# Attention of a 2-layer hybrid decoder step: a hand-written round of tasks and a planner that puts tasks out by predecessors, buffers and engine times

## The chip, the core and the metric

The kernel runs on one core of a Trainium2 chip. The metric is device time in microseconds (us), from the first to the last instruction plus what lies around it; the time of a kernel is the median of its runs. The engines are TensorE (PE in the profile; PEld is its weight load), VectorE (DVE), ScalarE (ACT), GpSimd (POOL) and SyncE (SP), which issues nearly all DMAs. Each engine takes its instructions in the order in which the program put them out, and waits on semaphores for the others.

## The reference, cut to what matters

One inference step for 256 new prompt tokens and 8 sequences of 4 sample tokens with 2,048 tokens of paged cache: two layers, each between two half-step SwiGLU FFNs. Layer 0 mixes by a short convolution, layer 1 by native sparse attention, whose three branches are a softmax over compressed blocks, one over the selected blocks and one over a window:

```python
def nsa_attend(q, t_pos, gates, k_cmp, v_cmp, gather_sel, kv_win, s_win):
    ...
    p_c = jax.nn.softmax(jnp.where(m_c, s_c, NEG), axis=-1) * m_c
    o_c = jnp.einsum('bqkgn,bnkd->bqkgd', p_c.astype(q.dtype), v_cmp)
    ...
    score = jnp.where(forced, FORCE_BONUS, jnp.where(valid, imp, -FORCE_BONUS))
    _, idx = lax.top_k(score, min(TOP_N, nb_s))
    k_sel, v_sel = gather_sel(idx)
    ...
    p_s = jax.nn.softmax(s_s.reshape(B, Tq, N_KV_HEADS, GROUP, n_sel * L_SEL), axis=-1)
    ...
    p_w = jax.nn.softmax(jnp.where(m_w, s_w, NEG), axis=-1)
    o_w = jnp.einsum('bqkgs,bskd->bqkgd', p_w.astype(q.dtype), kv_win[:, :, 1])
    o = gates[:, :, 0, ..., None] * o_c + gates[:, :, 1, ..., None] * o_s + gates[:, :, 2, ..., None] * o_w
```

All values are float32. The kernel computes the large products as three products of a high and a low part (`whi`, `wlo` of the weights, `xh`, `xl` of the activations).

## The kernel before

Prompt and sample tokens lie side by side (288 columns) in all projections and FFNs. The only stage that the change touches is the attention, between the last projection (queries) and `attention_out`; ahead of it and behind it the kernel is the same.

The attention has two kinds of work. The **sample** part goes over 20 chunks: for each of 4 pairs of sequences the window (`"w"`) and 4 chunks of the paged cache (0 to 3), each chunk 2 loads of 1 MB, one for each sequence of the pair. A chunk takes scores on PE (`s_scores`, `mm<-early,Qbd` and the like), mask and maximum on DVE (L1234), the exponential on ACT (L1235), four transposes on PE (`s_turn_p`, `tr<-ident,S`), a copy out of PSUM on ACT (L1248) and the values on PE (`s_values`, `acc<-early,PTs`). Chunks 0 to 3 need a mask `mk`, which a rank on PE (`s_rank`, `tr<-pcs,G`) and a chain of small DVE instructions make for each pair; at a pair's end stand small steps that weigh and add the parts (`s_weights` to `s_out`). The **prompt** part goes over 8 units of two heads: scores in two halves (`prompt_scores`, `mm<-kT,qT`), 8 exponentials on ACT, a scaling on POOL, 12 transposes, three copies, and values (`prompt_values`, `acc<-PcT,VcBig` and `acc<-PA,V`, `acc<-PB,V`).

PSUM has 8 banks: 4 `mm`, 2 `tr`, 2 `acc`. Before the attention the PSUM pool is closed and opened again with the same counts.

The pages' loads go into 12 buffers: 4 of the ring `raw` (which holds weights elsewhere), 4 `early`, and 4 pairs `whi`/`wlo` of the ring of converted weights, these until load 30 of 40. A load is issued on SP when the values of the chunk that had its buffer are put out; behind the last page the weights of `attention_out` are loaded into `raw`.

The order is written out by hand: a start (`START`) and then for every chunk the same round (`ROUND`), in which `i` takes prompt steps from a list at a pace of 0.8, `p` and `v` are turn and values of this chunk, `s` the scores of the next, and 0, 1, 2 places for the small steps (`HOOKS`). Steps on ACT and DVE that follow a PE step are put out after a guessed time (`soon`, `spend`). Near the end of the prompt list two weights of `attention_out` are converted, high part on ACT (L158), low part on POOL instead of DVE (L159). In the last prompt unit the scaling is shared by POOL and DVE.

Of the kernel before, what the change touches and what calls it, by code (L numbers as in the profile page):

```python
# [53 lines left out]

START = 'sSiiRC'
ROUND = 'i0p1si2v'
PACE = 0.8
KEEP = (7, 4, 2)
HOOKS = ((-5, 1), (-3, 1), (3, 2), (4, 2), (5, 0), (5, 2))
PT_ACT = 1  # L60
EARLY = (2, 1)
# [4 lines left out]
def weight_chunks():  # L66
# [35 lines left out]
    yield from ffn("ffb", 1)  # L102

# [83 lines left out]
def tile_step(ctx, tc, x_turned, vectors, state_turned, cmp_pages, sel_pages, cache_win, win_pages, page_table,  # L187
# [540 lines left out]
    def nsa(at):  # L728
# [10 lines left out]
        enter.enter_context(psum_banks(mm=4, tr=2, acc=2))  # L739
# [260 lines left out]


        clock, due, ties = [0.0], [], count()

        def soon(t, f, key):
            heappush(due, (clock[0] + t, next(ties), f, key))

        def run():
            t, _, f, _ = heappop(due)
            now, clock[0] = clock[0], t
            f()  # L1010
            clock[0] = max(now, t)

        def spend(t):
            end = clock[0] + t
            while due and due[0][0] <= end:
                run()
            clock[0] = end

        def need(key):
            while any(w[3] == key for w in due):  # L1020
                run()

        units = {}

        def prompt_cmp(u):
            if not u:
                units["cs"] = accb()
            pv = units["cs"][:, :256].rearrange("p (a u x) -> p a u x", a=2, u=KD)
            for a in range(2):
                mm(pv[:, a, u], qT[:, u, a * P:(a + 1) * P], KcBD[:, u // 4], True, True)  # L1030
            if u < KD - 1:
                return
            s = A("pc", [P, 2, 16, 8])
            sv = units.pop("cs")[:, :256].rearrange("p (a h n) -> p a h n", a=2, n=8)
            nc.vector.tensor_tensor(s, sv, cmN[:, :, None, :].to_broadcast([P, 2, 16, 8]), op=OP.add)
            m = A("pcm", [P, 2, 16])
            nc.vector.tensor_reduce(m, s, AX.X, OP.max)
            nc.vector.tensor_tensor(s, s, m[:, :, :, None].to_broadcast([P, 2, 16, 8]), op=OP.subtract)
            soon(1.6, lambda: nc.scalar.activation(s, s, AF.Exp, scale=SCALE), "cmp")
            soon(2.2, lambda: prompt_cmp1(s, m), "cmp")  # L1040
            units["cmp"] = s

        def prompt_cmp1(s, m):
            nc.vector.tensor_reduce(m, s, AX.X, OP.add)
            nc.vector.reciprocal(m, m)

            gv = gN[:, :, 0:16].rearrange("p a (pr kp g) -> p a pr g kp", pr=2, kp=2)
            for pr in range(2):
                mv = m[:, :, pr * 8:(pr + 1) * 8].rearrange("p a (g kp) -> p a g kp", kp=2)
                nc.vector.tensor_tensor(mv, mv, gv[:, :, pr], op=OP.mult)  # L1050
            nc.vector.tensor_tensor(s, s, m[:, :, :, None].to_broadcast([P, 2, 16, 8]), op=OP.mult)
            nc.vector.tensor_tensor(s, s, cm01[:, :, None, :].to_broadcast([P, 2, 16, 8]), op=OP.mult)
# [19 lines left out]

        enter.close()
        enter.enter_context(psum_banks(**ATT))
# [4 lines left out]
        K = {1: kT[2], 2: kT[4]}  # L1079
        PcT = T("PcT", [P, NP])  # L1080

        def prompt_cmp2():
            need("cmp")
            s = units.pop("cmp")
            ps = trb()
            for a in range(2):
                tr(ps[:, a * P:(a + 1) * P], s[:, a].rearrange("p h n -> p (h n)"))
            spend(0.2)
            nc.vector.tensor_copy(PcT, ps[:, :NP])

        def prompt_scores(u, half):

            pr, g = divmod(u, 4)
            if half == 0:
# [397 lines left out]
```

## Time and profile before

| | us |
|---|---|
| median of 3 runs | 1292.18 (1290.5 to 1292.75) |
| the profiled execution | 1289.71 |
| its span | 1288.0 |
| PE busy | 1249.7 (97%) |
| DVE, ACT, POOL busy | 724.8 (56%), 583.6 (45%), 251.1 (19%) |
| attention, from its first own matmul to the first of `attention_out` | 906.48 to 1037.44 |
| PE busy in 906.4 to 1037.4 | 108.32 of 131.00 |

The busy time is the union of an engine's instructions. Matmuls overlap each other (the next one starts before the end of the one ahead), so a piece of PE work costs the distance from its start to the start of the next piece, which is a little less than the busy time printed beside it. "PEclk" is the granted TensorE clock, 1.00 for the higher of its two levels (2.4 GHz) and 0.50 for the lower (1.2 GHz); values between are a mean over the stretch.

### The profile page before, as it was taken

What the parts mean: (1) busy time and instruction counts of PE and PEld (TensorE: products, weight loads), DVE (VectorE), ACT (ScalarE), POOL (GpSimd) and SP (SyncE); (2) the same over time, 40 slices, a digit from 0 to 9 for tenths busy, and PEclk for the clock granted to TensorE, in tenths of its full rate; (3) what the DMA queues carried; (4) which work ended last, traced back from release to release, by engine and by line L of the source; (5) the groups of instructions that cost most, each with busy time, mean ns of one, the idle gap of its engine ahead of it and who ended that gap; (6) DMA issues with size and microseconds to landing.
All of it is one profiled execution on the core that took longest, in us unless ns stands there. A gap on an engine that the chain in (4) does not pass through costs nothing.

```text
span 1288.0 us, 26738 instructions
## 1 busy us (share of the span) xinstructions
PE 1249.7 (97%) x10679; PEld 1193.7 (93%) x10679; DVE 724.8 (56%) x1394; ACT 583.6 (45%) x1050; POOL 251.1 (19%) x264
## 2 busy tenths in 40 slices
PE   9999999999999999999999999999888799999997
PEld 9999999999999999999999999999555489999997
DVE  6654455665664544656554555665667556645553
ACT  6433335543553433445443444542566445433444
POOL 0250122222212101212211021310112032210211
PEclk9999999999999999999999999999899999999999
DMA  7755555655555456456544543775697836665432
GB/s 269 274 202 183 195 192 178 241 204 184 194 201 183 169 201 250 156 189 230 196 167 145 197 152 107 282 267 181 212 369 260 320 135 227 253 245 196 152 104 77
DMA packets 71598, 262.07 MB, mean 203 GB/s; under 512 B 7985, under 2 KB 9906, under 8 KB 56242
## 3 DMA queue, kind: packets, MB, share of 16 engines
q1 hardware_dynamic: 70450, 249.66, 54.6%
q0 software_dynamic: 256, 8.32, 1.7%
q10 hardware_dynamic: 768, 2.38, 0.5%
q8 instruction: 84, 1.38, 0.4%
q14 instruction: 40, 0.33, 0.1%
HBM read 257.31 MB, written 11.35 MB: 209 GB/s over the span
## 4 chain that ended last, share of the span: by engine, by line
PE 85%; DVE 5%; ACT 4%; issue 2%; POOL 1%; SPq 1%; DMA 1%; ACTq 0%; DVEq 0%; POOLq 0%
PE mm L218 75%; PE acc L218 9%; PE tr L249 2%; DVE wlo L159 2%; ACT whi L158 1%; SPq L922 1%; DVE S L1108 1%; ACT sq L311 1%; ACT L449 0%; POOL t L683 0%; POOL a L464 0%; DMA raw<-in_sel_pages_dram 0%; ACT S L1109 0%; DMA wlo<-in_sel_pages_dram 0%; DVE PA L1141 0%
## 5 line engine op out<-in xcount | busy, mean ns | idle before, releaser
L218 PE MATMUL mm<-xh,whi 128*128 128x288 f32 x1832 | 546.4, 298 | 2.1 <-DVE xl L1158 0.9
L218 PE MATMUL mm<-xh,wlo 128*128 128x288 f32 x1832 | 543.0, 297 | 1.0 <-DVE wlo L159 1.0
L218 PE MATMUL mm<-xl,whi 128*128 128x288 f32 x1832 | 536.0, 293 | 0.0
L159 DVE TENSOR_TENSOR wlo<-raw,whi 128x1024 fp32r<-128x1024 f32 (+2 forms) x360 | 405.0, 1138 | 120.1 <-ACT whi L158 118.8
L158 ACT ACTIVATE whi<-raw 128x1024 fp32r<-128x1024 f32 (+2 forms) x365 | 343.1, 953 | 87.2 <-PE mm L218 81.2
L218 PEld LDWEIGHTS mm<-xh,whi 128*128 128x128 f32 x1832 | 343.9, 188 | 5.5 <-issue 1.8
L218 PEld LDWEIGHTS mm<-xl,whi 128*128 128x128 f32 x1832 | 347.9, 190 | 0.5 <-DVE xl L305 0.2
L218 PEld LDWEIGHTS mm<-xh,wlo 128*128 128x128 f32 x1832 | 342.9, 187 | 2.1 <-DVE wlo L159 1.9
L218 PE MATMUL mm<-Ah,wlo 128*128 128x288 f32 x768 | 228.7, 298 | 1.7 <-DVE wlo L159 1.7
L218 PE MATMUL mm<-Ah,whi 128*128 128x288 f32 x768 | 228.2, 297 | 1.5 <-ACT Ah L467 1.0
L218 PE MATMUL mm<-Al,whi 128*128 128x288 f32 x768 | 227.4, 296 | 0.4 <-DVE Al L468 0.4
L464 POOL TENSOR_TENSOR a<-s,t 128x288 f32<-128x288 f32 x88 | 114.9, 1305 | 492.9 <-DVE t L462 318.4
L218 PEld LDWEIGHTS mm<-Ah,whi 128*128 128x128 f32 x768 | 145.2, 189 | 2.4 <-ACT Ah L467 1.2
L218 PEld LDWEIGHTS mm<-Ah,wlo 128*128 128x128 f32 x768 | 144.3, 188 | 3.1 <-DVE wlo L159 3.1
L218 PEld LDWEIGHTS mm<-Al,whi 128*128 128x128 f32 x768 | 144.6, 188 | 0.6 <-DVE Al L468 0.6
L467 ACT ACTIVATE Ah<-a 128x288 fp32r<-128x288 f32 x88 | 39.2, 445 | 143.9 <-POOL a L464 143.7
L460 ACT ACTIVATE s<-t 128x288 f32<-128x288 f32 x88 | 39.1, 445 | 141.8 <-DVE t L458 141.6
L462 DVE TENSOR_TENSOR t<-mm,rB 128x288 f32<-128x288 f32 x88 | 40.1, 456 | 90.8 <-PE mm L218 90.7
L468 DVE TENSOR_TENSOR Al<-a,Ah 128x288 fp32r<-128x288 f32 x88 | 40.7, 462 | 68.5 <-ACT Ah L467 68.5
L498 DVE SCALAR_TENSOR_TENSOR xT<-mm,xT 128x288 f32<-128x288 f32 x64 | 29.2, 456 | 83.1 <-PE mm L218 83.1
L218 PE MATMUL acc<-cp,W 128*64 128x128 f32 x1024 | 59.4, 274 | 0.0
L218 PEld LDWEIGHTS acc<-cp,W 128*64 128x64 f32 x1024 | 55.6, 137 | 2.8 <-issue 2.8
(287 smaller groups left out, 885.6 us busy)
## 6 DMA issues: line engine op xcount, KB each, us to landing
raw<-in_w_ffb_gu_dram SPq DMA_DIRECT2D x44, 1024.0 KB
raw<-in_w_ffa_gu_dram SPq DMA_DIRECT2D x42, 1024.0 KB
cp<-in_cmp_pages_dram SPq DMA_DIRECT2D x128, 256.0 KB
early<-in_sel_pages_dram SPq DMA_DIRECT2D x56, 256.0 KB
raw<-in_sel_pages_dram SPq DMA_DIRECT2D x56, 256.0 KB
raw<-in_w_ffa_down_dram SPq DMA_DIRECT2D x16, 768.0 KB
raw<-in_w_conv_in_dram SPq DMA_DIRECT2D x12, 1024.0 KB
raw<-in_w_ffb_down_dram SPq DMA_DIRECT2D x16, 768.0 KB
```

The costliest lines, as they stand in the source:

```text
L158: self.nc.scalar.activation(parts[0], v, AF.Copy)
L159: (lower or self.nc.vector).tensor_sub(parts[1], v, parts[0])
L218: nc.tensor.matmul(out, lhsT, rhs, start=start, stop=stop, skip_group_check=True)
L249: nc.tensor.transpose(out, in_, ident[:k, :k])
L311: nc.scalar.activation(sq, xT[:, d], AF.Square)
L460: nc.scalar.activation(s1, t1, AF.Silu)
L462: nc.vector.tensor_mul(t2, pu[:, :N], rB)
L464: nc.gpsimd.tensor_mul(a, s1, t2)
L467: nc.scalar.activation(Ah[:, f], a, AF.Copy)
L468: nc.vector.tensor_sub(Al[:, f], a, Ah[:, f])
L498: nc.vector.scalar_tensor_tensor(xT[:, d], py[:, :N], 0.5, xT[:, d], op0=OP.mult, op1=OP.add)
L922: nc.sync.dma_start(v[:, s:s + 1], sel_pages[bass.ds(at_[s0 + s], 1)].rearrange("s p c -> p s c"))
```

## The change

The hand-written order goes: `START`, `ROUND`, `PACE`, `KEEP`, `HOOKS`, the heap of guessed times. Each step of the attention becomes a `Task` with an engine, a time from a table (`TAKES`), predecessors, slots of buffer rings that it takes or uses, and a rank. `Plan.run` keeps a clock for each engine, finds the task that can begin first, among the tasks of its engine that can begin within 0.1 us of it takes the one of the lowest rank, and puts it out. Loads are tasks on a queue of their own, 3.0 us each. Sample chunk `c` has the rank `c`, prompt unit `u` 3 + 2.2 `u`. The PSUM pool stays open from the projections on. `S`, which holds a chunk's probabilities, gets 3 buffers instead of 2.

Four steps are computed another way: the weights of a pair (`weights`) are exponentials with a bias, two on ACT, without the two subtractions on DVE (L1280) and without the memset; the mask `okp` is multiplied in once at the end; POOL scales the smaller part of a prompt unit first, and does all of it in the last unit too; three weights of `attention_out` are converted ahead instead of two, all with POOL for the low part.

```diff
-START = 'sSiiRC'
-ROUND = 'i0p1si2v'
-PACE = 0.8
-HOOKS = ((-5, 1), (-3, 1), (3, 2), (4, 2), (5, 0), (5, 2))
-EARLY = (2, 1)
+RINGS = dict(mm=4, tr=2, acc=2, U=2, PA=1, PB=1, S=3, PTs=2, small=2, pc=1, score=1, mk=2, sum=2, PTm=2)
+TAKES = dict(
+    small=0.5, max=0.75, parts=0.95, share=0.35, rank=0.25, best=1.25, S=1.0, top=0.65, top_w=0.75, exp=0.75, turn=0.5, copy=0.5,
...
+LOAD, LAND, HOP, FIRST_PAGES = 3.0, 1.5, 0.12, 7
+SAMPLE, PROMPT, PROMPT0, NEAR = 1.0, 2.2, 3.0, 0.1
+EARLY = 3
...
+    def start(self, t):
+
+        at = self.free.get(t.engine, 0.0)
+        for x in t.after:
+            if x.end is None:
+                return None
+            at = max(at, x.end + (0.0 if x.engine == t.engine else HOP))
+        taken = {}
+        for s in t.slots:
+            n = taken[s.ring] = taken.get(s.ring, -1) + 1
+            last = self.rings[s.ring][n]
+            for x in last.users if last else ():
+                if x.end is None:
+                    return None
+                at = max(at, x.end + HOP)
+        return at
+
+    def run(self):
+        left = list(self.tasks)
+        while left:
+            able = [(self.start(t), t) for t in left]
+            able = [(at, t) for at, t in able if at is not None]
+            first, t0 = min(able, key=lambda x: x[0])
+            at, t = min((x for x in able if x[1].engine == t0.engine and x[0] <= first + NEAR), key=lambda x: x[1].rank)
+            left.remove(t)
+            for s in t.slots:
+                self.rings[s.ring] = self.rings[s.ring][1:] + [s]
+            t.end = self.free[t.engine] = at + t.takes
+            t.put()
...
-        enter.enter_context(psum_banks(mm=4, tr=2, acc=2))
+        psum = at_pages.enter_context(ExitStack())
+        psum.enter_context(psum_banks(mm=4, tr=2, acc=2))
...
         enter.close()
-        enter.enter_context(psum_banks(**ATT))
...
-            late = u == KD - 1
-            n = 2 if late else 4
-            nc.gpsimd.tensor_tensor(S1[:, :n], S1[:, :n], sm[:, 0:n, None].to_broadcast([P, n, NP]), op=OP.mult)
-            (nc.vector if late else nc.gpsimd).tensor_tensor(S0, S0, sm[:, 4:8, None].to_broadcast([P, 4, P]), op=OP.mult)
...
+            f0 = step("POOL", "f1", lambda: scale(1), [f], uses=[sl["U"]], rank=r)
+            f1 = step("POOL", "f0", lambda: scale(0), [f0], uses=[sl["U"]], rank=r)
...
-            nc.vector.memset(w[:, 0:1], 0.0)
-            for k, sl in ((1, slice(1, 3)), (2, slice(3, 8))):
-                nc.vector.tensor_reduce(m2[:, k:k + 1], nb[:, sl], AX.X, OP.min)
-                ts(w[:, sl], nb[:, sl], m2[:, k:k + 1], None, op0=OP.subtract)
-            soon(0.6, lambda: nc.scalar.activation(w, w, AF.Exp, scale=-1.0), ("w", i))
...
+            def weights():
+                for k, at_ in ((1, slice(1, 3)), (2, slice(3, 8))):
+                    nc.scalar.activation(t["w"][:, at_], t["nb"][:, at_], AF.Exp, scale=-1.0, bias=t["m2"][:, k:k + 1])
...
+        before = values_of[:PAGES["until"] // 2]
+        for n in range(EARLY):
+            def convert():
+                W.convert(nc.gpsimd)
+                plan.free["POOL"] = max(plan.free.get("POOL", 0.0), plan.free["ACT"]) + 2.4
+            before = [step("ACT", "whi", convert, [*before, loads[len(order) + n // 2]], rank=100.0)]
```

What the change moves is shown at three places. The first is PE at the attention's start, from the first pair's compressed scores (`KcT`) on; `pcs` is what the rank reads, `pc` the prompt's compressed probabilities. Before:

```order
L218 MATMUL acc<-KcT,Qbd 32x64 x4
L218 MATMUL acc<-kT_9640,Qbd 32x32 x4
L218 MATMUL acc<-kT_9639,Qbd 32x32 x4
L218 MATMUL mm<-early,Qbd 32x512 x4
L218 MATMUL mm<-kT_9639,qT 128x256 x2
L218 MATMUL mm<-kT_9640,qT 128x256 x2
L218 MATMUL mm<-kT_9639,qT 128x128 x2
L218 MATMUL mm<-kT_9640,qT 128x128 x2
L218 MATMUL tr<-pcs,G 128x64
L249 MATMUL tr<-ident,pc 128x128 x2
```

Now, on the same engine and from the same place:

```order
L278 MATMUL acc<-KcT,Qbd 32x64 x4
L278 MATMUL acc<-kT_9640,Qbd 32x32 x4
L278 MATMUL acc<-kT_9639,Qbd 32x32 x4
L278 MATMUL mm<-early,Qbd 32x512 x8
L278 MATMUL mm<-raw,Qbd 32x512 x8
L278 MATMUL tr<-pcs,G 128x64
L309 MATMUL tr<-ident,pc 128x128 x2
```

Ahead of the rank there are now the scores of four chunks instead of those of one chunk and of the first prompt unit.

The second place is PE in the middle, around the second pair's rank. Before, from the prompt scores ahead of it to the transposes of the chunk that needs its mask (the second `tr<-ident,S`):

```order
L218 MATMUL mm<-kT_9640,qT 128x256 x2
L249 MATMUL tr<-ident,S 128x128 x4
L218 MATMUL tr<-pcs,G 128x64
L218 MATMUL mm<-raw,Qbd 32x512 x4
L218 MATMUL acc<-raw,PTs 32x128 x16
L218 MATMUL mm<-kT_9639,qT 128x128 x2
L218 MATMUL mm<-kT_9640,qT 128x128 x2
L249 MATMUL tr<-ident,S 128x128 x4
L218 MATMUL mm<-whi,Qbd 32x256 x4
```

Now, from the same rank on (`S_10906` and `S_10905` are the two halves of a prompt unit, `Vc` and `Sel` small steps of the first pair):

```order
L278 MATMUL tr<-pcs,G 128x64
L278 MATMUL mm<-early,Qbd 32x512 x4
L278 MATMUL acc<-Vc,sq 32x128 x4
L309 MATMUL tr<-ident,S 128x128 x4
L309 MATMUL tr<-ident,S_10906 128x128 x4
L278 MATMUL acc<-Sel,rB 128x64
L278 MATMUL acc<-whi,PTs 32x128 x8
L278 MATMUL acc<-wlo,PTs 32x128 x8
L309 MATMUL tr<-ident,S_10905 128x128 x8
L278 MATMUL mm<-early,Qbd 32x512 x4
L278 MATMUL acc<-PcT,VcBig 128x256
L278 MATMUL acc<-PA,V_10091 64x256 x2
```

The transposes of the chunk with the new mask moved behind all of these and the rest of that unit's values; the `tr<-ident,S` seen here belongs to the window chunk, which needs no mask.

The third place is the end. On PE the last rows before `attention_out` (`mm<-xh,whi`) were those of the last prompt unit:

```order
L218 MATMUL acc<-Sel,rms 128x64
L249 MATMUL tr<-ident,S_11983 128x128 x4
L249 MATMUL tr<-ident,S_11982 128x128 x8
L218 MATMUL acc<-PcT,VcBig 128x256
L218 MATMUL acc<-PA,V_10091 64x256 x2
```

Now they are those of the last two chunks and of the last pair's small steps:

```order
L278 MATMUL acc<-early,PTs 32x128 x16
L278 MATMUL mm<-raw,Qbd 32x512 x4
L309 MATMUL tr<-ident,S 128x128 x4
L278 MATMUL mm<-raw,Qbd 32x512 x4
L278 MATMUL acc<-raw,PTs 32x128 x16
L309 MATMUL tr<-ident,S 128x128 x4
L278 MATMUL acc<-raw,PTs 32x128 x16
L309 MATMUL tr<-ident,ssm 128x128
L278 MATMUL acc<-Vc,sq 32x128 x4
L278 MATMUL acc<-Sel,rms 128x64
L278 MATMUL mm<-xh,whi 128x288
```

The prompt's pieces that stood between the sample's last steps moved ahead of the last two chunks. On ACT at the same place (`S,L` are chunk exponentials, `PTs` and `sq` copies, `wg` the pair's weights, `xh` the output's high part, `whi` weights of `attention_out`) there stands now:

```order
L1340 ACTIVATE S,L<-S,nb 128x512
L1365 ACTIVATE Og<-acc 128x128
L1393 ACTIVATE wg<-nb,m_12539 128x2
L1393 ACTIVATE wg<-nb,m_12539 128x5
L1349 ACTIVATE PTs<-tr 128x512
L1414 ACTIVATE sq<-tr 128x128
L218 ACTIVATE whi<-raw 128x1024
L1447 ACTIVATE xh<-acc 128x8x8
L218 ACTIVATE whi<-raw 128x1024 x3
```

The first conversion, which came between prompt copies before, moved to the place just ahead of the output's last high part, and three more stand behind it.

## Rows read from the trace of the kernel before

**Rows 1.** Stretches: length, busy PE, PEld, DVE, ACT, POOL, PEclk, DMA share, GB/s.

```profile
906.40:1037.40 131.00, 108.32 (x1430) 68.25 (x1430) 81.64 (x388) 80.19 (x269) 25.23 (x20) 0.96 0.77 276
932.60:1001.00 68.40, 57.30 (x818) 36.80 (x810) 46.95 (x226) 44.47 (x155) 14.59 (x12) 1.00 0.88 311
1001.00:1037.40 36.40, 29.32 (x360) 17.90 (x360) 17.95 (x70) 18.05 (x50) 4.80 (x3) 0.95 0.72 271
916.00:920.00 4.00, 4.00 (x40) 1.40 (x38) 3.25 (x23) 4.00 (x18) 0.97 (x1) 0.50 0.00 0
956.00:960.00 4.00, 4.00 (x62) 2.98 (x58) 0.96 (x4) 1.48 (x4) 0.53 (x2) 1.00 1.05 385
```

**Rows 2.** Waits of PE, 905 to 1038: us in total, times, longest.

```profile
PE tr L249 <- ACT S L1235: 5.6, 5, 1.3
PE tr L218 <- DVE pcs L1193: 3.6, 1, 3.6
...
PE tr L249 <- DVE mm L1228: 2.1, 1, 2.1
...
PE acc L218 <- DVE pc L1035: 0.5, 1, 0.5
```

**Rows 3.** PE in order of time, 925 to 937: start, busy, what [idle before].

```profile
925.07 1.07 PE L218 MATMUL mm<-raw,Qbd 128*32 128x512 f32 x8
926.06 0.70 PE L218 MATMUL acc<-PcT,VcBig 128*128 128x256 f32 x2
...
928.14 1.08 PE L218 MATMUL acc<-early,PTs 128*32 128x128 f32 x32
929.15 1.14 PE L218 MATMUL mm<-kT,qT 64*128 64x256 f32 x8
...
932.84 0.72 PE L218 MATMUL mm<-kT,qT 64*128 64x128 f32 x8
934.85 0.66 PE L249 MATMUL tr<-ident,S 128*128 128x128 f32 x4 [1.29 <-ACT S L1235]
...
936.44 1.09 PE L249 MATMUL tr<-ident,S 128*128 128x128 f32 x8
```

**Rows 4.** PE in order of time at the attention's start.

```profile
913.28 0.41 PE L218 MATMUL tr<-pcs,G 128*128 128x64 f32 x2 [3.63 <-DVE pcs L1193]
...
913.92 2.76 PE L218 MATMUL mm<-kT,qT 64*128 64x256 f32 x8
```

**Rows 5.** ACT in order of time at the attention's start.

```profile
908.15 1.28 ACT L1183 ACT_TABLE_LOAD   x1 [18.05 <-DVE mm L1228]
...
910.36 0.40 ACT L1039 ACTIVATE pc<-pc 128x256 f32<-128x256 f32 x1
910.67 0.71 ACT L1235 ACTIVATE S<-S,nb 128x512 f32<-128x512 f32 x1
```

**Rows 6.** ACT by line, 906.4 to 1037.4: busy us, mean ns, idle before.

```profile
L1109 ACT ACTIVATE S<-S,mx 128x256 f32<-128x256 f32 (+1 forms) x64 | 28.2, 443 | 2.9 <-DVE mx L1108 2.9
L1248 ACT ACTIVATE PTs<-tr 128x512 f32<-128x512 f32 x20 | 11.9, 593 | 8.8 <-PE tr L249 8.8
```

**Rows 7.** DVE in order of time beside POOL, third pair's weights.

```profile
996.43 1.38 DVE L1280 TENSOR_SCALAR wg<-nb,m 128x2 f32<-128x2 f32 x1
```

**Rows 8.** POOL in order of time, the same stretch.

```profile
995.89 1.89 POOL L1124 TENSOR_TENSOR S<-S,sm 128x1024 f32<-128x1024 f32 x1 [10.53 <-DVE sm L1121]
```

**Rows 9.** PE at the end: values of the last chunk but one, `attention_out` begins.

```profile
1018.41 1.07 PE L218 MATMUL acc<-raw,PTs 128*32 128x128 f32 x24
...
1037.44 0.40 PE L218 MATMUL mm<-xh,whi 128*128 128x288 f32 x1 [0.94 <-DVE xl L1158]
```

**Rows 10.** SP in order of time at the end: weights of `attention_out`.

```profile
1019.33 6.03 SPq L138 DMA_DIRECT2D raw<-in_w_nsa_out_dram  x4
```

**Rows 11.** ACT in order of time at the end: first conversion.

```profile
1032.02 1.05 ACT L158 ACTIVATE whi<-raw 128x1024 fp32r<-128x1024 f32 x1
```

**Rows 12.** POOL in order of time at the end: its low part.

```profile
1033.15 2.35 POOL L159 TENSOR_TENSOR wlo<-raw,whi 128x1024 fp32r<-128x1024 f32 x1 [1.01 <-ACT whi L158]
```

More of the change, by code (lines that the diff above doesn't have):

```diff
@@ L102, in weight_chunks, with __init__, add @@
     yield from ffn("ffb", 1)
+class Task:
+    def __init__(self, engine, takes, put, after=(), slots=(), uses=(), rank=0.0):
+        self.engine, self.takes, self.put, self.after, self.slots, self.rank = engine, takes, put, after, slots, rank
+        self.end = None
+        for x in (*slots, *uses):
+            x.users.append(self)
+class Slot:
+    def __init__(self, ring):
+        self.ring, self.users = ring, []
+class Plan:
+    def __init__(self, rings):
+        self.rings = {n: [None] * k for n, k in rings.items()}
+        self.free, self.tasks = {}, []
+    def add(self, *a, **k):
+        t = Task(*a, **k)
+        self.tasks.append(t)
+        return t
+    def start(self, t):
[25 more added lines that the diff above has]
+            t.put()
 class Weights:
@@ new lines, in nsa, with nothing, step, load_more @@
+        landed = {}
+        U = [(u, *divmod(u, 4)) for u in range(KD)]
+        groups = [(b2 * 2 + pr, b2, pr) for b2 in range(2) for pr in range(2)]
+        def nothing():
+            pass
+        def step(engine, name, put, after=(), slots=(), uses=(), rank=0.0):
+            return plan.add(engine, TAKES[name], put, after, slots, uses, rank)
+        loads = [Task("DMA", 0, nothing) for _ in range(len(order) + 2)]
+        queue = [0.0]
+        def load_more(at):
+            n = len(pages) + len(done) + W.loaded - W.attention
+            load_pages()
+            for k in range(n, min(len(pages) + len(done) + W.loaded - W.attention, len(loads))):
+                queue[0] = max(queue[0], at) + LOAD
+                loads[k].end = queue[0] + LAND
@@ L1389, in nsa @@
-        while prompt:
-            item()
-        while due:
-            run()
+            puts = []
+            for n in range(3):
+                x = Slot("tr")
+                p = step("PE", "pturn", lambda n=n: turn(n), [(f0, f1, f1)[n]], [x], [sl["U"]], r - 0.2)
+                puts.append(step("DVE" if n == 1 else "ACT", "copy_v" if n == 1 else "copy", lambda n=n: put(n), [p] + puts[:1],
+                                 {0: [sl["PA"]], 2: [sl["PB"]]}.get(n, []), [x] + [sl["PA"]] * (n == 1), r - 0.2))
@@ L1393, in nsa @@
+        for n, x in enumerate(loads[:len(pages)]):
+            x.end = queue[0] = max(0.0, LOAD * (n + 1 - FIRST_PAGES))
+        plan.run()
         W.bufs = RAW
```

575 lines of the change are left out of this document (278 added, 297 removed).

## The prediction

> **What bounds the kernel now.** I read the busy times first, then the stretches of the attention, then who PE waits for. PE is busy for 1249.7 of 1288.0 us (the table of the profile), so outside the attention nothing can be won by another order. In the attention it is busy for 108.32 of 131.00 us, DVE for 81.64, ACT for 80.19 and the DMA queues for 0.77 of the time [rows 1]: no engine is full, PE is the nearest to it, and 22.7 us of its time are idle. The idle time is many short waits: 5.6 us for a chunk's exponential, 3.6 us for the first rank, 2.1 us ahead of a pair's turn [rows 2].
>
> I need the work that PE must do. A piece costs the distance to the next start [rows 3]: a chunk's scores 926.06 - 925.07 = 0.99, its values 1.01, its four transposes 0.66 less the overlap of 0.07 = 0.59; a prompt unit's scores 1.07 and 0.72 - 0.07 = 0.65, its 12 transposes 1.5 x 1.09 = 1.6, its values 928.14 - 926.06 = 2.08. 20 chunks x 2.59 = 51.8, 8 units x 5.40 = 43.2, and I estimate the small steps of four pairs and the first turn at 6.5 together: 101.5 us. So 131 - 101.5 = 29.5 us are lost, in idle time and at the lower clock.
>
> By stretch, counting the pieces in PE's order against the same prices: up to 932.6, 26.2 us hold 18.8 of work (7.4 lost); from there to 1001, 68.4 us [rows 1] hold 56.8 (11.6 lost); to 1037.4, 36.4 us hold 25.9 (10.5 lost). The first contains the one long wait, 3.63 us up to 913.28, and behind it the same eight score matmuls take 2.76 us that take 1.14 later [rows 3, 4]: the granted clock is 0.50 from 916 to 920 [rows 1], its lower level. PE had been idle just before.
>
> **The start: about 4 us won.** PE now has the scores of four chunks (4 x 0.99) ahead of the rank. On ACT the first exponential comes now before the parts of the first pair; the table load of 1.28 us then begins after DVE's third instruction on `pc`, some 0.8 us before the 908.15 of now [rows 5], and the rank can begin at about 911.7 instead of 913.28. PE's own work lasts until about 910.8, so the 3.63 us shrink to about 1, and I expect no fall of the clock there. Then ACT sets the pace. Up to the copy that the fourth chunk's values need it must do table load, three parts, five chunk exponentials (0.71 [rows 5] plus the read of the sum, 0.82 each as an estimate), four copies of 0.59 [rows 6], eleven prompt exponentials of some 0.44 [rows 6] and small steps, 15.7 us in all; with 3 us of waits for DVE it gets there at about 926. Followed piece by piece, PE has put out 22.6 us of work by 932.6, six chunks and two prompt units of scores, against 18.8 before: 3.8 us won. The end on the low side is 1.6 (the earlier rank alone), on the high side 6 (the lead that the same walk shows at 921, if ACT does not eat a part of it).
>
> The open PSUM scope is worth at most the 0.5 us for which the first score matmul waited on DVE's read of the old bank [rows 2]; it is inside the start.
>
> **The middle: 6 us won of 11.6.** The waits for the exponential of 1.29 us each have one pattern: rank, one chunk's scores, values, half a unit, then transposes that need the rank's mask [rows 3], as the second place shown ahead has it. That is 1.0 + 1.0 + 0.65 us of PE work over a chain of rank, DVE mask, maximum and exponential that takes some 4 us. In the new order over 8 us of other pieces stand in between, and the copies have a whole piece beside them. The two subtractions on DVE go too; at the third pair the first of them took 1.38 us [rows 7], under a POOL scaling of 1.89 us [rows 8]. The Trainium skill (SBUF — State Buffer, Who interferes with whom) says that DVE and GpSimd share a port pair that is locked for a whole instruction; the two rows fit it. By that rule the five `tensor_scalar`s that stay in the pair's weights could each still be held up under a scaling, up to 1.9 us for three pairs, which the sum leaves out, since those weights are not wanted at once.
>
> What stays is not zero. The table's costs are mostly within 0.1 us of the rows (scores 1.0 for 0.99, values 1.0 for 1.01, prompt values 2.05 for 2.08), but transposes stand at 0.5 for 0.59 and copies at 0.5 for 0.59, and the engines can't leave the order. A chunk's chain is so 0.2 us longer than planned, and PE has only two `tr` and two `acc` banks to run ahead in. Bounds for what is still lost in the middle: 2 us (only the table's errors show) and 11.6 us (as now). I take 5.5, 0.35 us a piece over some 16 chunk and unit pieces that are close to their copies, nearer to the lower end because the plan has the same rows' durations. Won: 6.1.
>
> **The end: nothing won.** All prompt work now stands ahead of the last two chunks. From the end of chunk 18's scores: its mask, maximum and exponential (0.78 + 0.87) with PE idle, transposes, scores of chunk 19, values, transposes of 19 (0.65 idle), its copy (0.7 idle), values, then weights (2.0 on DVE), a turn, a copy, small values, three small sums, the output and its two parts: 11.2 us, estimated with the same prices and 0.2 to 0.3 us for each small step, of which PE works 5.3. Before, 10.5 us were lost in the last stretch; now 5.9. Two things take this back. First, weights: their load is issued when chunk 18's values free `raw`, as now [rows 9, 10]: values from 1018.41, issue at 1019.33. Now only about 7 us follow, where 18 did. Two loads at the best rate of the trace, 385 GB/s [rows 1], need 2.7 us each, so with a second or two of issue and flight the first `whi` (1.05 us [rows 11]) begins about 4.5 us after the values, ACT holds it ahead of the last `xh`, and POOL's low part (2.35 us [rows 12]) ends some 12.4 us after the scores of chunk 18: PE stands for 1.3 us more. With POOL doing three low parts in a row, 7.1 us, PE's 2.4 us a piece follow them without a further stop. Second, PE works 5.3 us of 12.5, about as little as before 913, so I expect the lower clock at the start of `attention_out`, at the price of 913.28 to 920, some 3 us. The Trainium skill (TensorE: Matmul & The Clock Gate, What's actually happening) has the slow clock as the resting state that activity lifts; it speaks against a tail without prompt work. It can also stay high, as it does in the middle with its waits of 1.29 us. Lost at the end: 5.9 + 1.3 + 3 = 10.2, against 10.5. Bounds: 5.9 and 14 (a weight landing 4 us late).
>
> **Loads.** 28 of the 40 loads are issued inside the attention, 5.45 us a chunk at 385 GB/s. By the walk the first chunk's buffers come free at about 916, the fourth's at 928, and the last page then lands at about 1000, while PE needs it at about 1013. So the loads hold nothing up, with some 12 us to spare; at the 311 GB/s of the middle now [rows 1] it would be just in time.
>
> **The sum.** 3.8 + 6.1 + 0.3 = 10.2 us. Against the profiled execution (1289.71, of which 1288.0 are span): 1279.5. The median of the runs is 2.47 above it: 1282.
>
> **The rivals.**
> *ACT's fixed order takes the place of the waits (slower).* ACT now carries 64 prompt exponentials (28.2 us [rows 6]) between the chunks' exponentials and copies, in an order computed from costs that are too short. If a chunk's copy stands behind two to four prompt exponentials that wait themselves, PE stops with both `tr` banks full. It decides from 15.7 us lost in the middle on, 1.1 us for each of the 14 chunks; at the 1.29 us of now [rows 3] each, 18 us are lost and the kernel comes to 1294 to 1297. For it: at the start ACT really is the bound by my walk. Against it: ACT is busy for 44.47 of 68.40 us in the middle.
> *Loads bind.* If freed buffers come no faster than now, the last scores stand just ahead of 1018.41 again [rows 9], followed by the new tail: 4 us won at most, 1288.
> *The order does nothing on balance.* The waits go elsewhere, the same 29 us are lost, within 2 us of 1292. For it: the order before also keeps PE at 84% of the middle.
> *The plan holds well.* 2 us lost in the middle, no lower clock: 3.8 + 9.6 + 3.3 = 16.7, 1275.5; with the full lead at the start 1273.
>
> **How the numbers follow.** Forecast (1278 to 1287) 0.44; the plan holds well (under 1278) 0.20; loads bind or a small gain (to 1289.6) 0.11; nothing on balance 0.12; ACT (slower) 0.13. A measurement of this kernel can tell about 0.2%, 2.6 us, from no change. Faster 0.75, same 0.12, slower 0.13. Range 1273 to 1294, which leaves out about one in ten on either side.
>
> **What would show it.** Start: the wait ahead of the first `pcs` rank near 1 us, PEclk 1.00 in the stretch 906 to 926 after its start. Middle: waits of PE on the exponential under 2 us in total, PE busy near 92%. End: idle time between the last two chunks' scores and transposes, `whi` ahead of the last `xh` waiting for a DMA, PEclk under 1 at the start of `attention_out`. Wrong would be: PE waiting on ACT copies all through (ACT rival), or on DMA of pages, or `attention_out` beginning later than 1030.

## The result, and the profile after

| | before | after |
|---|---|---|
| median of 4 runs, us | 1292.07 (1290.5 to 1292.75) | 1277.15 (1275.35 to 1278.81) |
| the profiled execution | 1289.71 | 1278.04 |
| its span | 1288.0 | 1276.3 |
| attention, to the first matmul of `attention_out` | 130.94 | 113.75 |
| from there to the last of its sums of squares (`acc<-ss,ones`) | 32.66 | 36.85 |
| all that follows | 217.90 | 218.20 |

The ratio after to before is 0.9886, 95% interval 0.9868 to 0.9904: 14.9 us faster, where 10 were forecast. The attention became 17.2 us shorter, and `attention_out` gave 4.2 us back. The starts of these stretches are read to 0.1 us, so their lengths are good to about 0.05 us.

The first view is the stretches of the kernel after: time, then busy us and instructions of PE, PEld, DVE, ACT and POOL, then PEclk, the DMA share and GB/s. The attention is cut at the end of the first prompt unit's values (932.20) and of chunk 18's scores (1009.80); the last rows lie in `attention_out`.

```profile
907.50:932.20 24.70, 22.45 (x359) 14.63 (x358) 21.60 (x105) 18.72 (x70) 3.06 (x3) 1.00 0.78 270
932.20:1009.80 77.60, 72.29 (x983) 47.90 (x981) 47.93 (x240) 54.83 (x188) 20.26 (x17) 1.00 0.93 330
1009.80:1021.25 11.45, 5.41 (x95) 3.26 (x91) 5.57 (x25) 5.11 (x13) 0.34 (x1) 1.00 0.54 203
...
1020.00:1024.00 4.00, 1.33 (x7) 0.98 (x6) 0.22 (x1) 3.67 (x5) 3.09 (x2) 0.71 1.02 430
1024.00:1028.00 4.00, 4.00 (x18) 4.00 (x18) 2.43 (x1) 0.23 (x1) 4.00 (x2) 0.50 0.74 258
1028.00:1032.00 4.00, 4.00 (x31) 4.00 (x30) 0.46 (x1) 0.12 (x1) 0.92 (x1) 0.93 0.93 342
```

The idle time of PE is the difference of the first two numbers: 2.25 us in the start, 5.31 in the middle, 6.04 in the tail. In the middle PE is busy for 93% of the time, where the stretch before had 57.30 of 68.40 us, 84% [rows 1]. The clock is at its higher level all through the attention; before it fell behind the first rank [rows 1, 4] and once more in the last stretch (PEclk 0.95 from 1001.00 on [rows 1]). It falls now at the beginning of `attention_out`, down to 0.50 from 1024 to 1028.

The waits of PE from 905 to 1060 after (us in total, times, longest):

```profile
PE acc L278 <- DVE rms L1437: 3.0, 2, 1.6
PE tr L309 <- ACT S L1340: 2.5, 2, 1.7
PE mm L278 <- POOL wlo L219: 1.5, 1, 1.5
PE acc L278 <- DVE rB L1437: 1.3, 2, 0.7
```

Against [rows 2]: the five waits on a chunk's exponential (5.6 us) are down to two, both in the tail, and the 3.6 us for the first rank are gone from the top of the list. No PE wait on a page's load is among the waits. PE's own rows (start, busy, idle before and its releaser) show the first rank, then the tail and the beginning of `attention_out`:

```profile
912.09 0.41 PE L278 MATMUL tr<-pcs,G 128*128 128x64 f32 x2 [0.67 <-DVE mm L1330]
...
1011.53 0.65 PE L309 MATMUL tr<-ident,S 128*128 128x128 f32 x4 [1.67 <-ACT S L1340]
...
1019.72 0.41 PE L278 MATMUL acc<-Sel,rms 128*128 128x64 f32 x2 [1.33 <-DVE rms L1437]
...
1021.25 0.40 PE L278 MATMUL mm<-xh,whi 128*128 128x288 f32 x1 [1.13 <-DVE xl L1449]
...
1023.32 0.61 PE L278 MATMUL mm<-xh,wlo 128*128 128x288 f32 x1 [1.53 <-POOL wlo L219]
```

The weights of `attention_out` come late, as the rows of SP, ACT, POOL and DVE show:

```profile
1014.08 4.20 SPq L198 DMA_DIRECT2D raw<-in_w_nsa_out_dram  x4
...
1019.77 1.06 ACT L218 ACTIVATE whi<-raw 128x1024 fp32r<-128x1024 f32 x1 [1.87 <-DMA raw<-in_w_nsa_out_dram]
...
1020.91 8.01 POOL L219 TENSOR_TENSOR wlo<-raw,whi 128x1024 fp32r<-128x1024 f32 x3 [17.01 <-ACT whi L218]
...
1024.26 2.43 DVE L219 TENSOR_TENSOR wlo<-raw,whi 128x1024 fp32r<-128x1024 f32 x1 [3.06 <-ACT whi L218]
```

### The profile page after: what moved, and what is told of

Its sections match the earlier page's. It is cut to its first block, busy times and chain, and to the rows that moved or that the text cites. A ratio compares the mean times of both kernels' runs of the same rounds, so it can differ in the third digit from the quotient of the medians.

```text
span 1276.3 us, 26715 instructions
## 1 busy us (share of the span) xinstructions
PE 1244.7 (98%) x10679; PEld 1194.6 (94%) x10679; DVE 717.3 (56%) x1375; ACT 584.6 (46%) x1054; POOL 255.9 (20%) x266
## 3 DMA queue, kind: packets, MB, share of 16 engines
q10 hardware_dynamic: 768, 2.38, 0.5%
## 4 chain that ended last, share of the span: by engine, by line
PE 85%; DVE 5%; ACT 4%; POOL 2%; issue 2%; DMA 1%; SPq 0%; ACTq 0%; POOLq 0%; DVEq 0%
PE mm L278 76%; PE acc L278 8%; DVE wlo L219 2%; PE tr L309 2%; ACT whi L218 1%; ACT sq L371 1%; ACT L509 1%; POOL t L743 0%; DMA raw<-in_w_nsa_out_dram 0%; POOL S L1206 0%; DMA raw<-in_w_ffa_gu_dram 0%; SPq L983 0%; ACT S L1185 0%; DMA wlo<-in_sel_pages_dram 0%; DMA raw<-in_w_ffa_down_dram 0%
```

## The experiments

The question was which part of the change carries the gain, and what is still lost. The table has each kernel's median, its ratio to the kernel before on the same chip, and from its profiled execution the length of the attention with PE's idle time in it, and of `attention_out` up to the sums of squares. Not all kernels ran on one chip, and the kernel before took 1290.6 to 1292.1 us beside them; where two medians lie close, the ratios are the safer comparison.

| kernel | median, us | ratio (95%) | attention (idle) | `attention_out` |
|---|---|---|---|---|
| before | 1290.6 to 1292.1 | | 130.94 (22.6) | 32.66 |
| after | 1277.15 | 0.9886 (0.9868 to 0.9904) | 113.75 (13.6) | 36.85 |
| e_forms | 1294.65 | 1.0031 (1.0018 to 1.0044) | 137.44 (28.9) | 32.66 |
| e_psum_before | 1290.76 | 0.9998 (0.9989 to 1.0008) | 133.19 (24.3) | 32.71 |
| e_rank_first | 1304.38 | 1.0106 (1.0089 to 1.0123) | 142.90 (33.0) | 35.30 |
| e_act_cheap | 1287.53 | 0.9974 (0.9964 to 0.9983) | 127.38 (22.1) | 34.42 |
| e_until36 | 1280.16 | 0.9916 (0.9900 to 0.9933) | 119.66 (18.3) | 35.34 |
| e_fill | 1275.52 | 0.9885 (0.9869 to 0.9902) | 116.94 (8.0) | 32.76 |
| e_fill_short | 1276.52 | 0.9904 (0.9883 to 0.9926) | 113.59 (8.2) | 34.41 |
| e_costs_only | 1276.57 | 0.9889 (0.9872 to 0.9905) | 116.82 (16.2) | 35.18 |
| e_costs_only_q | 1270.13 | 0.9840 (0.9824 to 0.9857) | 111.94 (11.1) | 32.76 |
| e_load | 1270.48 | 0.9847 (0.9830 to 0.9863) | 111.59 (9.8) | 32.71 |
| e_load_q | 1270.28 | 0.9838 (0.9822 to 0.9855) | 112.58 (9.5) | 32.72 |
| e_costs_q | 1271.23 | 0.9855 (0.9831 to 0.9878) | 111.57 (9.1) | 32.73 |

### What carries the gain: the forms, the scope or the order

**e_forms.** The kernel before with its order written by hand, and with the change's other forms of the same computations, three `S` buffers and the open PSUM scope:

```diff
-            nc.vector.memset(w[:, 0:1], 0.0)
...
-                ts(w[:, sl], nb[:, sl], m2[:, k:k + 1], None, op0=OP.subtract)
...
+                    nc.scalar.activation(w[:, sl], nb[:, sl], AF.Exp, scale=-1.0, bias=m2[:, k:k + 1])
...
-            S = T("S", [P, 4, P], F32, 2)
+            S = T("S", [P, 4, P], F32, 3)
```

> The kernel before, its hand-written order kept, with the four changed computations alone (weights of a pair as two exponentials with a bias, okp once at the end, POOL scaling all of the last prompt unit with its smaller part first, three S buffers) and the PSUM pool left open. Theory (the order wins the time): only the 2.1 us wait ahead of the third pair's turn and the 0.5 us wait for the old bank go, and POOL's scaling of the last unit takes 0.7 us more near the end: 1289 to 1293 us, PE idle in the attention still 19 to 23 us. Rival (the computations win it): 1278 to 1283.

Measured: 1294.65 us, 0.3% slower than before and above the 1289 to 1293 that I gave, with 28.9 us of idle time where I expected 19 to 23. In the old order the forms carry nothing. (The third early conversion is not in this kernel, and no run has the planned order with the old forms.) Here the first rank's wait is as long as in [rows 2], the exponential is still waited for, and two pages come late:

```profile
PE tr L249 <- ACT S L1231: 5.2, 5, 1.2
PE tr L218 <- DVE pcs L1189: 3.6, 1, 3.6
...
PE mm L218 <- DMA raw<-in_sel_pages_dram: 3.1, 2, 2.1
```

**e_psum_before.** The kernel before with the open scope alone:

```diff
-        enter.enter_context(psum_banks(mm=4, tr=2, acc=2))
+        psum = at_pages.enter_context(ExitStack())
+        psum.enter_context(psum_banks(mm=4, tr=2, acc=2))
...
-        enter.enter_context(psum_banks(**ATT))
```

> The kernel before with the one PSUM scope only: the banks of the stage ahead of the attention stay open, no new scope is entered; the hand-written order stays. The prediction put this part at no more than 0.5 us, the wait of the first score matmuls on DVE's read of the old bank. Theory: that wait of 0.52 us goes, and the first rank's wait of 3.6 us stays or grows by it, because it hangs on DVE and ACT: 1290 to 1291 us, not to be told from the kernel before. Rival (the scope is what makes the early scores possible and carries some microseconds of the start): 1287 to 1289.

Measured: 1290.76 us, ratio 0.9998. PE's rows show why, against [rows 2, 4]: the first scores, which waited 0.5 us for DVE's `pc`, begin at once, 0.6 us earlier than before, and the rank comes no sooner.

```profile
905.87 0.32 PE L218 MATMUL acc<-KcT,Qbd 128*32 128x64 f32 x8
...
913.26 0.66 PE L218 MATMUL tr<-pcs,G 128*128 128x64 f32 x2 [3.63 <-DVE pcs L1193]
```

**e_rank_first.** The changed kernel, and the planner takes the task of lowest rank among all that can begin within 2.0 us of the first, instead of 0.1:

```diff
-SAMPLE, PROMPT, PROMPT0, NEAR = 1.0, 2.2, 3.0, 0.1
+SAMPLE, PROMPT, PROMPT0, NEAR = 1.0, 2.2, 3.0, 2.0
```

> The changed kernel with NEAR 2.0 instead of 0.1: the planner takes the task of lowest rank among those that can begin within 2 us of the first, so an engine is made to wait for up to 2 us in the plan where it could do something else. Theory (the gain is that what can begin first goes first): PE idle in the middle rises from some 4 to 8 to 12 us, 1281 to 1287. Rival (any sensible interleaving with the same ranks does as well, since the waits of the order before came from a few bad places): 1276 to 1279.

Measured: 1304.38 us, 27 us slower than the changed kernel and slower than the order written by hand; I had the direction, and the size far too small. PE's waits name the place, prompt transposes that are put in PE's queue ahead of work that could have begun:

```profile
PE tr L309 <- POOL S L1206: 16.2, 14, 2.7
PE acc L278 <- ACT PTs L1349: 5.6, 10, 0.7
```

The attention is 29 us longer: PE's idle time rises by 19.4 us, and the rest is PE's own work, longer at the lower clock (PEclk 0.74 from 906 to 926, where the kernel after has 1.00). The same tasks, times, buffers and forms give 1277 or 1304 us. With e_forms and e_psum_before, which gain nothing, this shows that the order carries the gain and that the rule of choice decides over it: here an engine that works off its queue in a fixed order was given tasks that wait while another could run.

**e_act_cheap.** The slower rival made strong: most of ACT's times in the planner's table halved.

```diff
-... S=1.0, top=0.65, top_w=0.75, exp=0.75, turn=0.5, copy=0.5,
+... S=1.0, top=0.65, top_w=0.75, exp=0.37, turn=0.5, copy=0.25,
```

> ACT's times in the planner's table are halved (exponential 0.37, copies 0.25, prompt exponentials 0.25 and 0.2, parts 0.47), so that its order is computed from costs that are far too short: the slower rival of the prediction, made strong. If the engines' fixed order is sensitive to such errors, PE waits on ACT's copies and exponentials for some 1 us a chunk, 10 to 20 us more than the changed kernel: 1287 to 1297. If the bounded banks and the ranks carry most of the order, whatever the costs, 2 to 6 us more: 1279 to 1283.

Measured: 1287.53 us, 10.4 over the changed kernel, at the low end of what I gave for an order sensitive to costs. The mechanism of the rival exists: PE waits for ACT's copies and exponentials,

```profile
PE acc L278 <- ACT PTs L1349: 5.7, 6, 2.4
PE tr L309 <- ACT S L1340: 4.6, 4, 1.7
```

10.3 us where the changed kernel has 3.2 (0.7 and 2.5). But it takes costs at half their size; with errors of 0.1 us a step, as the table of the kernel after has them, PE waits 3.2 us for these steps.

### What is left in the tail

**e_until36.** The ring `split` serves pages until load 36 instead of 30, so that `raw` comes free sooner and the weights' load is issued earlier:

```diff
-PAGES = dict(early=4, split=4, until=30)
+PAGES = dict(early=4, split=4, until=36)
```

> The changed kernel with one number changed: pages may go into the ring of converted weights until load 36 instead of 30, so that the last two chunks lie in `early` and `raw` is free for the weights of attention_out some 15 us sooner. Theory (the end is bound by these weights): ACT's first conversion waits for no DMA, PE's 1.5 us wait for POOL's low part goes and the 1.1 us wait for the output's low part falls to 0.6: 2 to 3 us less than the changed kernel, 1274 to 1276. The lower clock at the start of attention_out stays. Rival (the wait is hidden by the clock's or by other work): as the changed kernel, 1277.

Measured: 1280.16 us, slower than the changed kernel by 3; both theories missed. The load is early (issued at 996.43 instead of 1014.08), `whi` waits for no DMA and `attention_out` for no low part. But POOL now makes its low parts while DVE makes the last pair's weights. Rows of POOL, DVE and PE:

```profile
1014.66 4.64 POOL L219 TENSOR_TENSOR wlo<-raw,whi 128x1024 fp32r<-128x1024 f32 x2 [12.47 <-ACT whi L218]
```
```profile
1014.67 2.37 DVE L1404 TENSOR_SCALAR wg<-wg,fg 128x5 f32<-128x5 f32 x1
1016.96 2.41 DVE L1406 TENSOR_SCALAR ssm<-ssm,fg 128x64 f32<-128x64 f32 x1
```
```profile
1019.80 0.45 PE L309 MATMUL tr<-ident,ssm 128*128 128x128 f32 x1 [5.99 <-DVE ssm L1406]
```

The 128x5 instruction takes 0.23 us in the kernel after. Here each of the two lasts until one of POOL's two subtractions (2.32 us each) has ended, and PE stands for 6 us. The clock falls behind that wait (PEclk 0.50 from 1020 to 1028).

**e_fill and e_fill_short.** Matmuls on a matrix of ones, whose result nobody reads, put into PE's idle places of the tail: 40, and then 21 that are shorter than the waits they lie in.

```diff
+        def fill_pe(n):
+            w = mmb()
+            for _ in range(n):
+                mm(w[:, :P], ones, ones, True, True)
...
+                    if (i, j) == (3, 2):
+                        fill_pe(6)
```

> The changed kernel with 40 matmuls more on constants into free banks (128 columns, results unused), put into PE's five idle places between the last two chunks' scores and attention_out. Theory (the tail's idle time lowers the clock, which costs 2.4 us at the start of attention_out): PEclk 1.00 from 1020 to 1032, 2 to 2.5 us less, 1274.5 to 1275.5, the waits for whi and wlo as they were. Rival (the clock follows something else, or the fillers delay the tail): clock 0.5 in 1024 to 1028 as now, 1277 to 1279.

> The fillers of the run with 40 matmuls on a matrix of ones, cut to 21 and placed so that each group is shorter than the wait it lies in (6 behind chunk 18's scores, 3 behind its values, 3 behind chunk 19's transposes, 5 behind the last small values, 4 behind the last output). Theory (the low clock at the start of attention_out comes from PE's idle tail and costs 2 to 2.5 us): the tail is no longer than the 11.4 us of the changed kernel, PEclk 0.9 to 1.00 from 1020 on, and 1.5 to 2.5 us less than the changed kernel, 1274 to 1276. Rival (PE must work nearly all the tail, as with 40 fillers, for the clock to stay): PEclk falls to 0.50 for some microseconds again, 1276.5 to 1278.

Measured: 1275.52 and 1276.52 us. By time neither can be told from the changed kernel; the four runs of e_fill_short spread from 1273.85, the profiled one, to 1281.86, and their mean granted clock from 0.997 to 0.993 (0.994 and 0.995 in the four of the kernel after). The stretch 1024 to 1028, first of e_fill, then of e_fill_short, answers the question on the clock:

```profile
1024.00:1028.00 4.00, 4.00 (x32) 4.00 (x31) 1.50 (x1) 0.00 (x0) 3.76 (x2) 1.00 0.81 289
```
```profile
1024.00:1028.00 4.00, 4.00 (x32) 4.00 (x32) 1.31 (x2) 0.32 (x1) 3.12 (x1) 1.00 0.80 301
```

PEclk is 1.00 in both where the kernel after has 0.50, so the median of e_fill_short lies in the rival's range and its clock is the theory's. In the profile of e_fill_short the attention is as long as after (113.59 for 113.75), the wait for `wlo` is there (1.46 us), and `attention_out` takes 34.41 instead of 36.85 us: the clock's price is 2.4 us. With 40 fillers the attention is 3.2 us longer, since they run past the waits. That the medians don't show the 2.4 us stays open: only the profiled executions have a trace.

### What is left in the middle, and a better version

**e_costs_only.** Thirteen times of the table (the text below says ten) set to the rows of the trace:

```diff
-... S=1.0, top=0.65, top_w=0.75, exp=0.75, turn=0.5, copy=0.5,
+... S=1.0, top=0.72, top_w=0.92, exp=0.85, turn=0.6, copy=0.61,
...
```

> Ten engine times of the planner's table are set to the rows (transposes 0.5 to 0.6, copies 0.5 to 0.61, exponential 0.75 to 0.85, maxima 0.65 to 0.72 and so on); the load time stays at 3.0. The prediction gave 5.5 us lost in the middle to transposes and copies that the table has too short. By that theory PE's idle time in the attention falls by 1.5 to 3 us: 1273 to 1276 us. Rival (the 3.5 us measured there come from other places, where chains and banks leave nothing to put in between): the idle time in the middle stays at 3 to 4 us, and the time changes only by what the other order does in the tail, 1275 to 1279.

(The 3.5 us of that text are counted against 101.5 us of work; as idle time the middle of the kernel after has 5.31, as above.) Measured: 1276.57 us. In 932 to 1010 PE is busy for 71.64 of 78.00 us, 6.4 idle: better times in the table take nothing off the middle. That is the rival's case. The order puts prompt work into the tail, which should have helped, and a new wait took it back. Rows of DVE, POOL and PE:

```profile
1011.97 7.25 DVE L1421 SCALAR_TENSOR_TENSOR rms<-Og,wg,rms 128x128 f32<-128x128 f32 x3
```
```profile
1012.00 7.06 POOL L219 TENSOR_TENSOR wlo<-raw,whi 128x1024 fp32r<-128x1024 f32 x3 [2.43 <-ACT whi L218]
```
```profile
1019.82 0.65 PE L278 MATMUL acc<-Vc,sq 128*32 128x128 f32 x8 [5.14 <-DVE rms L1433]
```

Three sums that take 1.13 us after take 7.25, with POOL's three low parts beside them: one sum for each low part, as in e_until36.

**e_costs_only_q.** The same order, with each early low part on POOL cut into four subtractions of 128x256:

```diff
-        (lower or self.nc.vector).tensor_sub(parts[1], v, parts[0])
         nk = v.shape[1]
+        for k in range(0, nk, nk // cut):
+            at = slice(k, k + nk // cut)
+            (lower or self.nc.vector).tensor_sub(parts[1][:, at], v[:, at], parts[0][:, at])
```

> The run with the ten corrected engine times, with one edit more: each of the three early low parts on POOL (128x1024) is cut into four subtractions of 128x256; the order of PE, ACT and DVE is the same. In the run without the cut DVE's three sums on SBUF operands took 7.25 us beside POOL's 7.06 us of low parts (1.13 us in the kernel before and after), and PE stood 5.1 us for them. Theory (a DVE instruction whose operands are all in SBUF waits for the end of the POOL instruction under way, so that the hold has the length of one POOL instruction): the three sums take 1.1 to 3 us and PE's wait falls to under 2 us, 3 to 5 us less in all, 1271.5 to 1274. Rival (DVE gets its turn only when POOL has nothing queued, whatever the length of a piece): the sums take some 7 us again and the time stays, 1275.5 to 1278.

Measured: 1270.13 us, 6.4 less than without the cut and below the 1271.5 to 1274 that I gave. The attention is 4.9 us shorter and `attention_out` 2.4, since with the wait the lower clock behind it goes too (PEclk 1.00 instead of 0.50 from 1020 to 1028). DVE, then POOL:

```profile
1011.73 2.38 DVE L1423 SCALAR_TENSOR_TENSOR rms<-Og,wg,rms 128x128 f32<-128x128 f32 x3
```
```profile
1011.76 9.49 POOL L222 TENSOR_TENSOR wlo<-raw,whi 128x256 fp32r<-128x256 f32 x12 [2.43 <-ACT whi L218]
```

The hold has the length of one POOL instruction: 0.79 us a piece, and the sums take 0.79 each (2.38 for three). POOL pays 9.49 us instead of 7.06, and PE never waits for POOL's low parts. The Trainium skill (SBUF — State Buffer, Who interferes with whom) states that a DVE instruction with two SBUF inputs contends with a GpSimd instruction that reads SBUF, and calls the shared port pair an exclusive lock; these sums, 0.79 us each beside POOL's pieces and 0.38 without them, agree.

**e_load.** The planner's time for one load, 3.0 us, set to 2.75:

```diff
-LOAD, LAND, HOP, FIRST_PAGES = 3.0, 1.5, 0.12, 7
+LOAD, LAND, HOP, FIRST_PAGES = 2.75, 1.5, 0.12, 7
```

> The planner's time for one page load is set from 3.0 to 2.75 us; nothing else. In its order the last prompt unit's transposes and values then stand between the last two chunks and in the last pair's steps, where the changed kernel has no prompt work. My theory (loads have slack, and what is left to win lies in the empty tail): from the scores of chunk 18 to the first matmul of attention_out PE works over 9 of some 12 us instead of 5.4 of 11.4, PEclk stays at 1.00 or close to it at the start of attention_out, no wait on a page; 1272 to 1275 us. Rival (loads are nearly due, and a planner that believes in faster ones asks for chunks too early): PE waits on raw pages for 3 us or more, 1278 to 1283.

Measured: 1270.48 us, 6.7 less than the changed kernel (5.0 by the ratios, whose two intervals don't touch) and below the 1272 to 1275 that I gave. No wait on a page is among PE's waits. From the end of chunk 18's scores (998.10) to `attention_out` PE works for 15.59 of 18.89 us, so 3.3 us are idle where the kernel after has 6.04; the clock stays at 1.00 there, and `attention_out` takes its 32.71 us. Between the profiled executions that is 4.1 us of the gain, and the attention gives 2.2. The last 14 us before `attention_out`:

```profile
1003.00:1016.99 13.99, 10.69 (x144) 6.94 (x140) 10.81 (x41) 10.99 (x32) 6.54 (x4) 1.00 0.62 249
```

Now the last unit's transposes begin at 1011.84 and its values at 1013.42, inside the last pair's steps. By the planner's rule the reason is that 3.0 us a load made the last chunks come late in its plan, so that it worked off all prompt work ahead of them; the plan's own times are not on record, so this is argued and not shown. In the trace after, from 946 to 986, a load took about 2.8 us (1.05 MB at 379 and 367 GB/s). The clock does fall once in the middle of e_load, after waits of 0.75, 0.37, 1.27 and 0.19 us:

```profile
984.00:988.00 4.00, 4.00 (x29) 1.65 (x23) 2.78 (x16) 3.86 (x17) 0.00 (x0) 0.67 1.05 386
```

Two chunks' scores take 1.93 and 1.84 us there instead of 1.06, so this order has some 1.6 us left to win.

**e_load_q and e_costs_q.** The cut of e_costs_only_q added to e_load, and to both corrections.

> The run with LOAD = 2.75, with the same cut of POOL's early low parts into four. There the own-row mask on DVE took 1.67 us (0.29 alone) under POOL's first low part. Theory of the hold for one POOL instruction: it takes 0.3 to 0.9 us now and attention_out begins 0.5 to 1.3 us earlier, 1269 to 1270 us. Rival (a longer sum of pieces: POOL's fixed cost for each subtraction and the wait of attention_out for wlo eat it): 1270 to 1271.5.

> Corrected engine times and LOAD = 2.75 and the cut together. If the two corrections add (less idle time in the middle, prompt work in the tail, no long hold): 1267 to 1269.5 us. If the middle has no more to give, as PE's idle time of 6 to 7 us there in the two runs with one correction each says: the same as LOAD = 2.75 alone, 1269.5 to 1271.5.

Measured: 1270.28 and 1271.23 us. The own-row mask is held for less (0.72 us instead of 1.67 in e_load), but the attention is no shorter; the corrections don't add. Two things stand beside that in the traces: in e_load_q the clock falls in the middle as in e_load (PEclk 0.70 from 984 to 988), and in e_costs_q PE waits for pages (1.3 and 0.5 us), as in no other planned order here. e_load, one number changed, and the cut with the corrected times are both 5 to 7 us better than the changed kernel and 20 better than the kernel before; between them these runs can't choose.

## Why the prediction was right, and where its sizes were off

The direction, the mechanism and the range held. The forecast for the profiled execution was 1279.5 and it took 1278.04; for the median it was 1282, 4.9 us too much. The median lies just below the forecast's own stretch of 1278 to 1287, in the one that was given 0.20 for a plan that holds well. Step by step, what was lost, in us:

| step | forecast | measured |
|---|---|---|
| start, left | 3.6 | 2.25 |
| middle, left | 5.5 | 5.31 |
| tail, PE idle | 5.9 | 6.04 |
| wait for `wlo` | 1.3 | 1.53 |
| lower clock in `attention_out` | 3 | 2.4 |
| work of PE | 101.5 | 100.15 busy |

**The start.** The rank's wait was to shrink to about 1 us and is 0.67; PEclk was to stay and did. ACT was to set the pace, 22.6 us of work by 932.6; PE is busy for 22.45 us by 932.20. That ACT sets it is not borne out: of PE's 2.25 us idle time in the start only 0.7 end with ACT, the rest with DVE. Of the open scope I said 0.5 us at most: e_psum_before shows 0.6 us at the first scores, and nothing of it in the time while the rank is late.

**The middle.** The size was right and the reason was not. I gave the 5.5 us to transposes and copies that the table has too short. With the table corrected the idle time is 6.4 us, so the size was luck. What the trace after has there instead are waits at the joints of work: 1.6 and 1.3 us for the own-row mask of a pair ahead of its last product, 1.0 for POOL's scaling, 0.9 for a copy on DVE (PE's waits from 932.2 to 1009.8). One of the masks is itself held by POOL:

```profile
991.01 2.89 POOL L1206 TENSOR_TENSOR S<-S,sm 128x512 f32<-128x512 f32 x2 [8.71 <-PE mm L278]
```
```profile
992.92 1.13 DVE L1437 TENSOR_TENSOR rB<-rB,okp 128x128 f32<-128x128 f32 x1
```
```profile
994.10 0.43 PE L278 MATMUL acc<-Sel,rB 128*128 128x64 f32 x2 [0.70 <-DVE rB L1437]
```

The mask takes 0.29 us when POOL is idle. I had this hold in the text for the weights' `tensor_scalar`s, and left it out because nobody waits for them at once; for the mask somebody does, by 0.70 us.

**The end.** The tail of 11.2 us is 11.45, and both prices behind it were there: the late weights with 1.53 us for the low part, and the lower clock with 2.4, as e_fill_short has it. One size on the way was off: the first `whi` begins 6.8 us after the start of chunk 18's values (1013.00 to 1019.77) and not 4.5; PE stands for little more than forecast, since it does two other products first. I took the tail for a property of the change. It is one of the numbers in the plan: with `LOAD` at 2.75, or with the corrected table, the planner keeps prompt work for it, and with `LOAD` at 2.75 idle tail, late low part and lower clock go together. I gave the loads 12 us to spare; in the trace after, the DMA share is 0.47 from 1004 to 1008 and 0.00 from 1008 to 1012, and chunk 19's scores begin at 1012.11, so it is about 6. I did not ask what the planner does with a load time that is too long.

**The sum.** Up to the end of `attention_out` the kernel was 3.4 us better than my terms have it: 1.35 in the start, 0.6 by the scope (which I had inside the start), 1.35 since PE's work is less than I had estimated, 0.1 in the rest. The profiled execution gave 1.6 of it back in its first 16 us, which the change does not touch, and 0.3 behind `attention_out`. The stretches 0 to 16, of before and of after:

```profile
0.00:16.00 16.00, 14.89 (x88) 13.80 (x89) 9.30 (x16) 11.91 (x18) 0.44 (x5) 1.00 0.88 354
```
```profile
0.00:16.00 16.00, 13.20 (x73) 12.58 (x74) 8.77 (x16) 11.47 (x18) 0.44 (x5) 0.89 0.89 345
```

After, PE waits there for the first `xh`, and not before:

```profile
7.13 0.83 PE L278 MATMUL mm<-xh,whi 128*128 128x288 f32 x2 [1.70 <-ACT xh L362]
```

In e_load, whose program is the same there, this stretch has PEclk 1.00 again. What missed most is the last step: I set the median 2.47 us above the profiled execution, as before, and it lies 0.9 below. That is 3.4 of the 4.9 us. One execution's distance from the median is chance, and should not have been carried over to another kernel.

**The rivals.** ACT's fixed order: its mechanism is real (e_act_cheap) but was seen only with costs at half their size. Loads bind: no page is waited for; they do bind a little in e_forms, 3.1 us, and in e_costs_q, 1.8 us. Nothing on balance: refuted by the idle time, 13.6 us for 22.6. The plan holds well: nearest to the time measured, though not by its terms, since the lower clock and the late low part were there.

## What to carry to other kernels

In this kernel, engines with queues in a fixed order gained from a planner that gives each the task that can begin first: with the same tasks and costs a planner that prefers rank over readiness lost 27 us against it. Look at what the planner believes about resources that are not short, here the loads: 0.25 us less for a load filled the tail, though PE waited for no page without that step or with it. Where POOL and DVE both read SBUF, cut POOL's long instructions that may run beside a chain on DVE: 2.4 us more on POOL took 6.4 us off e_costs_only, where PE waited for that chain, and nothing off e_load, where the hold was 1.4 us.

## What the runs showed of the hardware

A DVE instruction on five columns took 2.37 us instead of 0.23 because a POOL subtraction of 128x1024 was under way, and three sums took 7.25 instead of 1.13. DVE instructions with one operand in PSUM were not held: in e_load the low part of `xl` (from `acc`) took its 0.42 us at 1016.03 as elsewhere, inside POOL's low parts, while the mask before it, with both operands in SBUF, took 1.67 instead of 0.29:

```profile
1013.34 8.09 POOL L219 TENSOR_TENSOR wlo<-raw,whi 128x1024 fp32r<-128x1024 f32 x3 [2.65 <-ACT whi L218]
```
```profile
1014.19 1.67 DVE L1437 TENSOR_TENSOR rms<-rms,okp 128x128 f32<-128x128 f32 x1
1016.03 0.42 DVE L1248 TENSOR_TENSOR xl<-acc,xh 128x256 fp32r<-128x256 f32 x1 [0.17 <-ACT xh L1247]
```

And the clock fell within `attention_out`, while PE had work, after a tail in which it was busy for 5.41 of 11.45 us. In the first 16 us of that execution it fell too, after the wait of 1.70 us that ended at 7.13: PEclk is 0.89 over these 16 us, and 1.00 in the other thirteen profiled executions, where the same wait is 0 to 1.1 us.
